# Seven-product blocks of a feed-forward stage: the plain product on the lower left weights third, the outputs of the block ahead in front of the sixth product

## The chip, the cores and the metric

The kernel runs on one core of one Trainium2 chip. The metric is the device time of one execution in microseconds, the median of several runs. All times below are in microseconds unless marked ns.

## The reference

A decoder trunk of two layers over 256 tokens of width 1024. Each layer is a feed-forward network (FFN), an attention, and a second FFN; the first layer's attention is of the stick-breaking kind, the second's a sliding window of 128 with sinks, whose keys and values come from the stream after the first layer. The FFN, which this study is about, is

```
def swiglu(x, w_in, w_out):
    gate, up = jnp.split(x @ w_in, 2, axis=-1)
    return (jax.nn.silu(gate) * up) @ w_out

h = h + 0.5 * swiglu(rms_norm(h, norm), w_in, w_out)     # four times
```

with `w_in` of 1024 x 5632 and `w_out` of 2816 x 1024, all float32. The four FFNs are most of the work.

## The kernel before

**Precision.** Every float32 weight is split into two parts: ACT casts it to `w_hi` (L418), DVE subtracts that from the original and writes the rest as `w_lo` (L420), each in two halves of 128 x 1024. Operands are split the same way (`xT`, `S_h` and `S_l`, `aT_h` and `aT_l`). A *step* is three matmuls of 128 x 512 (operand high on w_hi, operand low on w_hi, operand high on w_lo). A product has four steps.

**Blocks.** An FFN goes through its 2816 hidden columns in blocks. The first blocks are of a plain or a narrow kind; the others, 512 columns wide, use Strassen's scheme, in which the two token tiles, the two halves of the 1024 inputs and gate and up form a 2 x 2 by 2 x 2 product. Four weight tiles of 1 MB are loaded for such a block, r11 and r21 (gate, upper and lower half of the inputs; r21 holds the lower left weights) and r12 and r22 (up). Seven products replace eight. The first FFN has four such blocks, the other three five each, 19 in all. The numbers by which the code calls the products are used here: before the change they run in the order 1, 5, 3, 2, 6, 7, 4.

- Product 1: r11, plain, into PSUM bank a. Its result is copied for later use, in most blocks into bank b (L797).
- DVE adds r12 to r11 (`add`, L610). Product 5: r11 on the operand sum S0, into bank d. ACT copies the result to the tile p5 (`stage`, L781).
- Product 3: r22 on S3, added into bank d.
- Product 2: r21, plain, into bank b. ACT's silu of that gives the gate s1 of the first token tile.
- Product 6: r11 (by then r11 + r12 + r22) on S1, added into bank a. ACT copies bank a to u2; DVE adds bank d to u2 (`plus`, L785) and multiplies with s1 (L788); PE transposes the result (L676), ACT and DVE split it into aT_h and aT_l.
- Product 7: r12 (by then r12 + r22) on S2, added into bank a. DVE adds bank a to p5 (`plus`, L785).
- Product 4: r11, plain, added into bank a; silu of that times p5 is the second token tile's half.

The sum r12 + r22, and the lower left weights that are added to r11 for product 4, are made by an accumulating DMA from POOL's queue (`fetch`, L615); the other two sums are made by DVE.

**Outputs.** A finished block's aT_h and aT_l are multiplied with two 1 MB tiles of `w_out` in 16 steps (8 for a narrow block) that accumulate over the FFN in four banks. `between()` places the output steps of the block ahead; before the change it stands between product 7 and product 4. The last two blocks' outputs stand behind the last block.

**Order.** Each instruction is recorded as a task with a duration, a place and what it reads and writes; a list planner then decides the order on each engine. PE's tasks have the order of the code as their rank, but when the first in rank isn't ready, PE takes the next that is. Hence a piece of a later product or of the outputs can stand between two products. Tasks of other engines are ranked by when they are due. The resulting order is fixed when the program is built; on the chip each engine's queue waits at its first instruction that isn't ready. Weight tiles pass through six raw slots and ten slots (five pairs) for w_hi and w_lo; a slot is handed on in the order of the code.

Of the kernel before, what the change touches and what calls it, by code (L numbers as in the profile page):

```python
# [18 lines left out]
D = 1024  # L19
# [20 lines left out]
PIECES = 2  # L40
ADDING = 170.0
PLAIN = 330.0
BY_DMA = False
DMA3 = True
FSUMS = 5000.0
TM = 1000.0
BOOST = 10000.0
# [11 lines left out]
LATE = (True, True, True)  # L59
KVFIRST = True  # L60
KVLATE = 3000.0
C11_0 = False
BL_LATE = 0.0

# [149 lines left out]
def dve(n):  # L214
    return n / 0.96 + 70
# [11 lines left out]
def kernel(  # L227
# [34 lines left out]
    RAW, WP, A4 = Slots("raw", RAWS, 8), Slots("w", HL, 8), Slots("a", 4, 4)  # L262
# [17 lines left out]
    def ts(t):  # L280
        return slice(t * P, (t + 1) * P)
# [7 lines left out]
    def B(*bs):  # L289
        return [(b, 0) for b in bs]  # L290
# [109 lines left out]
    def flat(buf):  # L400
        return buf.ap.rearrange("p a b -> p (a b)")
# [3 lines left out]
    def split(raw, prio=None):  # L405
        prio = plan.pos - LEAD if prio is None else prio
        a, b = raw.ab
        if raw.cut == 4:
            return split_fine(raw, prio)
        hi, lo = WP.get([P, a, b], F32R, "w_hi"), WP.get([P, a, b], F32R, "w_lo")  # L410
        m = a * b // PIECES
        for j in range(PIECES):
            sl = slice(j * m, (j + 1) * m)
            ks = [j] if PIECES == 2 else [0, 1]
            rs = [2 * j, 2 * j + 1] if raw.cut == 4 else ks

            first = [(xh, (0, 0))] if raw.cut == 4 and j == 1 else []
            T("ACT", act(m), lambda sl=sl: ACT.copy(out=flat(hi)[:, sl], in_=flat(raw)[:, sl]),  # L418
              r=[(raw, i) for i in rs] + first, w=[(hi, i) for i in ks], prio=prio)
            T("DVE", dve(m), lambda sl=sl: DVE.tensor_sub(out=flat(lo)[:, sl], in0=flat(raw)[:, sl],  # L420
                                                          in1=flat(hi)[:, sl].bitcast(F32)),
              r=[(raw, i) for i in rs] + [(hi, i) for i in ks], w=[(lo, i) for i in ks], prio=prio)
        return hi, lo
# [22 lines left out]
    def by_k(w):  # L446
        return w.rearrange("(k p) n -> p k n", p=P)
# [23 lines left out]
    def of_x(t, k):  # L471
        return ((lambda: xh.ap[:, k, ts(t)], lambda: xl.ap[:, k, ts(t)]), [(xh, (t, k // 4)), (xl, (t, k // 4))])
# [129 lines left out]
    def of_sums(SH, SL, i):  # L602
        return lambda kk: ((lambda: SH.ap[:, i, kk], lambda: SL.ap[:, i, kk]), [(SH, i), (SL, i)])

    def add(dst, src):
        m = 2048 // PIECES
        for i in range(PIECES):
            sl = slice(m * i, m * i + m)
            ks = [i] if PIECES == 2 else [0, 1]
            T("DVE", dve(m), lambda sl=sl: DVE.tensor_add(out=flat(dst)[:, sl], in0=flat(dst)[:, sl], in1=flat(src)[:, sl]),  # L610
              r=[(src, k) for k in ks], w=[(dst, k) for k in ks], prio=plan.pos - LEAD)


    def fetch(dst, src):
        T("POOL", 1500, lambda: nc.gpsimd.dma_start(out=dst.ap, in_=src, accum_op=ALU.add), w=[(dst, 0), (dst, 1)],  # L615
          prio=plan.pos - LOADS, lat=500.0)
        T("SP", P * 2048 * 4 / ADDING, lambda: None, w=[(dst, 0), (dst, 1)], prio=plan.pos - LOADS)

    def product(bank, raw, xs, first, last, at=0.0):
        w = split(raw)  # L620
        for kk in range(4):
            step(bank, w, kk, xs(kk), first and kk == 0, last and kk == 3)
        WP.put(*w)

    def ffn(w_in, w_out, acc, rest, finish, kv=None, blocks=BLOCKS, roots=None, ending=False, there=False, arranged=False):

        first, late = arranged, roots is not None
        wi, wo = by_k(w_in), by_k(w_out)  # L630
        wi4 = w_in.rearrange("(j p k) n -> p j k n", j=2, k=4)
        ring = [banks[i] for i in rest[0:3]]
# [16 lines left out]
        def of_s(i):  # L649
            return of_sums(SH, SL, i)  # L650

        def col(h, i, c, n=512):
            cs = slice(h * DFF + c, h * DFF + c + n)
            return wi4[:, i, :, cs] if first else wi[:, 4 * i:4 * i + 4, cs]

        def silu(dst, src, r, w, t, n=512):
            if late:
                T("ACT", act(n, True), lambda: ACT.activation(out=dst(), in_=src(), func=AF.Silu, scale=roots[t][0].ap), r=r + B(roots[t][0]) + [(consts, "tbl")], w=w)
            else:
                T("ACT", act(n), lambda: ACT.activation(out=dst(), in_=src(), func=AF.Silu), r=r + [(consts, "tbl")], w=w)  # L660
# [9 lines left out]
        def turn(m, t, aT, nk=4):  # L670
            n = nk * P
            view = lambda b: (lambda: b.ap[:, 0:nk, ts(t)])

            def run():
                for i in range(nk):
                    PE.transpose(out=tr.ap[:, i * P:(i + 1) * P], in_=m.ap[:, i * P:(i + 1) * P], identity=ident)  # L676
            T("PE", 109 * nk, run, r=B(m) + ID, w=B(tr))
            STG.put(m)
            part_to(tr, (aT[0], t, view(aT[0])), (aT[1], t, view(aT[1])), n,
                    lambda: tr.ap[:, 0:n].rearrange("p (a b) -> p a b", a=nk))  # L680
# [92 lines left out]
        def strassen(n, c, between):  # L773
            a, d, b = ring
            ring[:] = [d, b, a]
            aT = new_a()
            r11, r12, r22, r21 = [load([(slice(0, 512), col(h, i, c))], 4, 512) for h, i in ((0, 0), (1, 0), (1, 1), (0, 1))]

            def stage(src, name):
                s = STG.get([P, 512], F32, name)  # L780
                T("ACT", act(512), lambda: ACT.copy(out=s.ap, in_=src.ap), r=B(src), w=B(s), prio=plan.pos - STAGE)  # L781
                return s

            def plus(s, bank):
                T("DVE", dve(512), lambda: DVE.tensor_add(out=s.ap, in0=s.ap, in1=bank.ap), r=B(bank), w=B(s))  # L785

            def mul_less(dst, a_, b_, r, w, t):
                T("DVE", dve(512), lambda: DVE.scalar_tensor_tensor(out=dst(), in0=b_(), scalar=roots[t][1].ap if late else -1.0, in1=a_(),  # L788
                                                                    op0=ALU.mult, op1=ALU.mult),
                  r=r + (B(roots[t][1]) if late else []), w=w, lat=LAT["DVE"] + TM)  # L790

            product(a, r11, lambda kk: of_x(0, kk), True, False)
            c11 = C11 and (n != 1 or blocks[0] == "p" or C11_0)
            if c11:
                T("ACT", act(512), lambda: ACT.copy(out=b.ap, in_=a.ap), r=B(a), w=B(b), prio=plan.pos - STAGE)  # L797
                s1 = STG.get([P, 512], F32, "s1")
            else:
                s1 = stage(a, "s1")  # L800
            add(r11, r12)
            product(d, r11, of_s(0), True, False)
            p5 = stage(d, "p5")
            if BY_DMA:
                fetch(r11, col(1, 1, c))
            else:
                add(r11, r22)
            if DMA3:
                fetch(r12, col(1, 1, c))
            else:  # L810
                add(r12, r22)
            product(d, r22, of_s(3), False, True)
            RAW.put(r22)
            product(b, r21, lambda kk: of_x(0, 4 + kk), not c11, True)
            RAW.put(r21)
            if c11:
                silu(lambda: s1.ap, lambda: b.ap, B(b), B(s1), 0)
            else:
                plus(s1, b)
                silu(lambda: s1.ap, lambda: s1.ap, [], B(s1), 0)  # L820
            product(a, r11, of_s(1), False, False)
            fetch(r11, col(0, 1, c))
            u2 = stage(a, "u2")
            plus(u2, d)
            mul_less(lambda: s1.ap, lambda: s1.ap, lambda: u2.ap, B(u2), B(s1), 0)
            STG.put(u2)
            turn(s1, 0, aT)
            product(a, r12, of_s(2), False, False)
            RAW.put(r12)
            plus(p5, a)  # L830
            between()
            product(a, r11, lambda kk: of_x(1, 4 + kk), False, True)
            RAW.put(r11)
            m = STG.get([P, 512], F32, "m")
            silu(lambda: m.ap, lambda: a.ap, B(a), B(m), 1)
            mul_less(lambda: m.ap, lambda: m.ap, lambda: p5.ap, B(p5), B(m), 1)
            STG.put(p5)
            turn(m, 1, aT)
            return aT, 4
# [300 lines left out]
    def shared_kv(vec, other):  # L1140
# [25 lines left out]
        def run(ring, tr):  # L1166
# [19 lines left out]
            at_ = plan.pos  # L1186
            plan.pos += KVLATE
            for t in range(NT):
# [404 lines left out]
```

## Time and profile before

| | |
|---|---|
| median of 3 runs | 911.37 (910.37 to 911.4) |
| the profiled execution, and its span | 910.39, span 908.6 |
| first FFN, 19 to 185 | PE busy 166.00 of 166.00, DVE 148.04, DMA 0.93 |
| second FFN, 290 to 475 | PE 185.00 of 185.00, DVE 174.79, DMA 0.86 |
| third FFN, 475 to 662 | PE 186.44 of 187.00, DVE 174.90, DMA 0.89 |
| fourth FFN, 722 to the end | PE 178.97 of 186.60, DVE 171.46, DMA 0.74 |

PE is the engine of the matrix products (PEld its weight loads), DVE and ACT the vector and scalar engines, POOL and SP issue DMAs. A row of the timeline holds the start, the length, the engine, the line of the kernel, the operation, the output and inputs by their names in the program, and in brackets how long the engine stood idle before and what ended that. Two tiles are called p and u there: p5 and u2 with their numbers left out. A matmul's end is modelled, so consecutive matmuls overlap in the rows, and a short wait is seen in the distance of their starts.

### The profile page before, as it was taken

The page shows a single profiled execution, that of the slowest core. Times are in us where ns is not written, and L with a number is a line of the kernel's source. Part 1 is how long each engine was busy: PE and PEld are TensorE (multiplying, and loading weights), DVE is VectorE, ACT ScalarE, POOL GpSimd, SP SyncE. Part 2 cuts the span into 40 slices and gives each one's busy share as a digit, 9 for nine tenths or more (in the row PEclk, how much of TensorE's full clock was granted, in tenths as well). Part 3 has the DMA queues.
Part 4 walks back from the last instruction along what each step waited for, and adds up shares of the span by engine and source line. Part 5 has one row for each costly group of instructions (what it writes and reads, how often), then busy time and mean ns, then how long its engine had stood idle before and what let it go on. Part 6 is the DMA issues. An engine that isn't in the chain of part 4 may idle for free.

```text
span 908.6 us, 11840 instructions
## 1 busy us (share of the span) xinstructions
PE 897.5 (99%) x4420; PEld 739.5 (81%) x4420; DVE 818.3 (90%) x989; ACT 650.1 (72%) x935; POOL 66.7 (7%) x71
## 2 busy tenths in 40 slices
PE   9999999999999999999999999999999999999997
PEld 6888888888888888888888878888897787788886
DVE  8989989687977999998889999999788799999985
ACT  7867667786986876776688767667857677677662
POOL 2001000000000101010000101010000001101000
PEclk9999999999999999999999999999999999999999
DMA  9997999995763499999795999998944149999951
GB/s 337 349 238 223 289 298 233 285 291 154 239 206 115 104 267 306 246 290 268 211 343 127 255 264 266 284 318 225 335 129 163 47 107 287 284 250 291 323 148 47
DMA packets 107305, 214.43 MB, mean 236 GB/s; under 512 B 6256, under 2 KB 27760, under 8 KB 107248
## 3 DMA queue, kind: packets, MB, share of 16 engines
q1 hardware_dynamic: 85184, 170.49, 52.6%
q0 software_dynamic: 21648, 42.99, 26.9%
q8 instruction: 34, 0.56, 0.2%
q10 hardware_dynamic: 416, 0.20, 0.1%
q14 instruction: 23, 0.19, 0.1%
HBM read 212.62 MB, written 1.05 MB: 235 GB/s over the span
## 4 chain that ended last, share of the span: by engine, by line
PE 89%; DVE 8%; ACT 2%; issue 1%; DMA 0%; DVEq 0%; ACTq 0%
PE ps L287 85%; DVE w_lo L420 4%; PE ps L676 2%; ACT w_hi L418 1%; PE ps L490 1%; DVE raw L610 1%; DVE e L1319 0%; PE ps L1327 0%; DMA hN<-in_x_dram 0%; DVE s L586 0%; DVE small L1293 0%; DVE S_l L580 0%; ACT u L781 0%; DVE aT_l L497 0%; DVE o_l L1359 0%
## 5 line engine op out<-in xcount | busy, mean ns | idle before, releaser
L420 DVE TENSOR_TENSOR w_lo<-raw,w_hi 128x1024 fp32r<-128x1024 f32 x424 | 499.8, 1219 | 24.7 <-ACT w_hi L418 23.1
L418 ACT CAST w_hi<-raw 128x1024 fp32r<-128x1024 f32 x424 | 423.0, 1049 | 102.9 <-DVE raw L610 40.0
L287 PE MATMUL ps<-w_hi,xT 128*128 128x512 f32 (+1 forms) x788 | 229.8, 375 | 0.0
L287 PEld LDWEIGHTS ps<-w_hi,xT 128*128 128x128 f32 x788 | 142.7, 188 | 26.6 <-DVE xT L497 0.5
L287 PE MATMUL ps<-w_lo,xT 128*128 128x512 f32 (+1 forms) x394 | 146.8, 373 | 0.0
L287 PE MATMUL ps<-w_hi,aT_h 128*128 128x512 f32 x354 | 139.9, 395 | 0.0
L287 PE MATMUL ps<-w_lo,aT_h 128*128 128x512 f32 x354 | 137.7, 389 | 0.0
L287 PE MATMUL ps<-w_hi,aT_l 128*128 128x512 f32 x354 | 137.5, 388 | 0.0
L287 PE MATMUL ps<-w_hi,S_h 128*128 128x512 f32 x320 | 127.3, 398 | 2.0 <-ACT u L781 1.2
L287 PE MATMUL ps<-w_lo,S_h 128*128 128x512 f32 x320 | 124.9, 390 | 0.0
L287 PE MATMUL ps<-w_hi,S_l 128*128 128x512 f32 x320 | 124.8, 390 | 0.0
L610 DVE TENSOR_TENSOR raw<-raw 128x1024 f32<-128x1024 f32 x78 | 94.6, 1220 | 0.5
L615 POOL DMA_DIRECT2D raw<-in_ffn_w_in_dram x38 | 48.3, 1271 | 507.2 <-DVE w_lo L420 255.3
L287 PEld LDWEIGHTS ps<-w_lo,xT 128*128 128x128 f32 x394 | 74.2, 188 | 13.6 <-DVE w_lo L420 0.4
L287 PEld LDWEIGHTS ps<-w_lo,aT_h 128*128 128x128 f32 x354 | 66.4, 188 | 13.9
L287 PEld LDWEIGHTS ps<-w_hi,aT_l 128*128 128x128 f32 x354 | 66.6, 188 | 13.0
L287 PEld LDWEIGHTS ps<-w_hi,aT_h 128*128 128x128 f32 x354 | 66.5, 188 | 12.8
L287 PEld LDWEIGHTS ps<-w_hi,S_h 128*128 128x128 f32 x320 | 60.1, 188 | 16.8 <-ACT u L781 3.2
L287 PEld LDWEIGHTS ps<-w_lo,S_h 128*128 128x128 f32 x320 | 60.1, 188 | 13.0 <-DVE w_lo L420 0.2
L287 PEld LDWEIGHTS ps<-w_hi,S_l 128*128 128x128 f32 x320 | 60.2, 188 | 11.5
L496 ACT CAST aT_h<-ps 128x512 fp32r<-128x512 f32 (+1 forms) x48 | 26.3, 549 | 49.4 <-PE ps L676 49.2
L287 PE MATMUL ps<-xT,w_hi 128*128 128x512 f32 (+1 forms) x136 | 47.0, 394 | 0.0
(184 smaller groups left out, 941.7 us busy)
## 6 DMA issues: line engine op xcount, KB each, us to landing
raw<-in_ffn_w_in_dram SPq DMA_DIRECT2D x76, 1024.0 KB, 7.5
raw<-in_ffn_w_out_dram SPq DMA_DIRECT2D x44, 1024.0 KB, 8.2
raw<-in_ffn_w_in_dram POOLq DMA_DIRECT2D x38, 1024.0 KB, 10.0
raw<-in_sb_w_qkv_dram SPq DMA_DIRECT2D x12, 1024.0 KB, 8.0
raw<-in_ffn_w_in_dram SPq DMA_DIRECT2D x16, 512.0 KB, 6.4
raw<-in_ffn_w_in_dram SPq DMA_DIRECT2D x16, 256.0 KB, 5.4
raw<-in_sb_w_o_dram SPq DMA_DIRECT2D x4, 1024.0 KB, 5.3
raw<-in_swa_w_q_dram SPq DMA_DIRECT2D x4, 1024.0 KB, 9.0
```

What stands on the lines that cost most here:

```text
L287: PE.matmul(ps, lhsT=lhsT, rhs=rhs, start=start, stop=stop, skip_group_check=True)
L418: T("ACT", act(m), lambda sl=sl: ACT.copy(out=flat(hi)[:, sl], in_=flat(raw)[:, sl]), r=[(raw, i) for i in rs] + first, w=[(hi, i) for i i ...
L420: T("DVE", dve(m), lambda sl=sl: DVE.tensor_sub(out=flat(lo)[:, sl], in0=flat(raw)[:, sl], in1=flat(hi)[:, sl].bitcast(F32)), r=[(raw, i) ...
L490: PE.matmul(bank.ap[:, i * P:(i + 1) * P], lhsT=s, rhs=ident, start=i == 0, stop=True, is_transpose=True, skip_group_check=True)
L496: T("ACT", act(n), lambda: ACT.copy(out=hi[2](), in_=src()), r=B(bank), w=[hi[0:2]])
L610: T("DVE", dve(m), lambda sl=sl: DVE.tensor_add(out=flat(dst)[:, sl], in0=flat(dst)[:, sl], in1=flat(src)[:, sl]), r=[(src, k) for k in ks ...
L615: T("POOL", 1500, lambda: nc.gpsimd.dma_start(out=dst.ap, in_=src, accum_op=ALU.add), w=[(dst, 0), (dst, 1)], prio=plan.pos - LOADS, lat=5 ...
L676: PE.transpose(out=tr.ap[:, i * P:(i + 1) * P], in_=m.ap[:, i * P:(i + 1) * P], identity=ident)
```

## The change

A table `SPECIAL`, keyed by the FFN and the block, gives for each seven-product block who makes the four sums (V for DVE, D for an accumulating DMA), which of products 2 and 3 goes first, and in front of which product the outputs of the block ahead stand. All 19 blocks get the same entry. The makers stay as they were. Product 2 goes third and product 3 fourth, and `between()` stands in front of product 7 instead of product 4. The products now run in the order 1, 5, 2, 3, 6, (outputs), 7, 4. The raw slots of r21 and r22 are handed on in the new order too.

```diff
-BY_DMA = False
-DMA3 = True
...
+SPECIAL = {(f, n): ('VVDD', (2, 3), 7) for f in (1, 2, 3, 4) for n in range(1, 6)}
...
-            add(r11, r12)
+            makers, second, filled = SPECIAL.get((len(stage_), n), ("VVDD", (3, 2), 4))
+
+            def fill(q):
+                if q == filled:
+                    between()
...
+            summed(0, r11, r12, 1, 0)
             product(d, r11, of_s(0), True, False)
             p5 = stage(d, "p5")
...
-            product(d, r22, of_s(3), False, True)
-            RAW.put(r22)
-            product(b, r21, lambda kk: of_x(0, 4 + kk), not c11, True)
-            RAW.put(r21)
+            summed(1, r11, r22, 1, 1)
+            summed(2, r12, r22, 1, 1)
+            for q in second:
+                if q == 3:
+                    product(d, r22, of_s(3), False, True)
+                    RAW.put(r22)
+                else:
+                    product(b, r21, lambda kk: of_x(0, 4 + kk), not c11, True)
+                    if makers[3] == "D":
+                        RAW.put(r21)
...
+            fill(6)
             product(a, r11, of_s(1), False, False)
-            fetch(r11, col(0, 1, c))
+            summed(3, r11, r21, 0, 1)
...
             turn(s1, 0, aT)
+            fill(7)
             product(a, r12, of_s(2), False, False)
             RAW.put(r12)
             plus(p5, a)
-            between()
+            fill(4)
             product(a, r11, lambda kk: of_x(1, 4 + kk), False, True)
```

(Lines L286, L419, L496, L609, L787 and L790 of the changed kernel are L287, L420, L497, L610, L785 and L788 of the one before.) What the planner makes of it, on PE, in the second seven-product block of the fourth FFN. Before, product 3 (w_hi_6283) follows product 5 (w_hi_6304) at once:

```order
L287 MATMUL ps_66<-w_hi_6304,S_h_6099 128x512
L287 MATMUL ps_66<-w_hi_6304,S_l_6117 128x512
L287 MATMUL ps_66<-w_lo_6320,S_h_6099 128x512
L287 MATMUL ps_66<-w_hi_6283,S_h_6099 128x512
L287 MATMUL ps_66<-w_hi_6283,S_l_6117 128x512
L287 MATMUL ps_66<-w_lo_6359,S_h_6099 128x512
```

and now, after product 5 (w_hi_6312), the ahead block's product 4 (w_hi_6341):

```order
L286 MATMUL ps_66<-w_hi_6312,S_h_6099 128x512
L286 MATMUL ps_66<-w_hi_6312,S_l_6117 128x512
L286 MATMUL ps_66<-w_lo_6325,S_h_6099 128x512
L286 MATMUL ps_66<-w_hi_6341,xT_163 128x512 x2
L286 MATMUL ps_66<-w_lo_6355,xT_163 128x512
```

Four steps of it, and only then product 3; in most other blocks the four steps are product 2's, of which two stood there before. Further on in the same block, on PE before, product 7 (w_hi_6411) behind product 6 (w_hi_6406):

```order
L287 MATMUL ps_66<-w_hi_6406,S_h_6099 128x512
L287 MATMUL ps_66<-w_hi_6406,S_l_6117 128x512
L287 MATMUL ps_66<-w_lo_6423,S_h_6099 128x512
L287 MATMUL ps_66<-w_hi_6411,S_h_6099 128x512
L287 MATMUL ps_66<-w_hi_6411,S_l_6117 128x512
L287 MATMUL ps_66<-w_lo_6451,S_h_6099 128x512
```

and now, behind product 6 (w_hi_6395), output steps (aT), nine in all up to product 7:

```order
L286 MATMUL ps_66<-w_hi_6395,S_h_6099 128x512
L286 MATMUL ps_66<-w_hi_6395,S_l_6117 128x512
L286 MATMUL ps_66<-w_lo_6413,S_h_6099 128x512
L286 MATMUL ps_66<-w_hi_6363,aT_h_6293 128x512
L286 MATMUL ps_66<-w_hi_6363,aT_l_6400 128x512
L286 MATMUL ps_66<-w_lo_6423,aT_h_6293 128x512
```

Between products 7 and 4, where 14 output steps and the transpose of s1 stood in a block in the middle of an FFN, there are now steps of the next block's product 1: two in three blocks, three in ten (and three output steps in one), and more, of either kind, in five.

On DVE, in the second seven-product block of the second FFN, the add to p5 stood before behind the u2 and s1 operations and the split of a `w_out` tile (w_hi_2922), far ahead of product 4's split (w_hi_2993):

```order
L785 TENSOR_TENSOR u2_2936<-u2_2936,ps_66 128x512
L788 SCALAR_TENSOR_TENSOR s1_2911<-u2_2936,small_67,s1_2911 128x512
L497 TENSOR_TENSOR aT_l_2829<-ps_66,aT_h_2772 128x4x128
L420 TENSOR_TENSOR w_lo_2957<-raw_2859,w_hi_2922 128x1024 x2
L785 TENSOR_TENSOR p5_2861<-p5_2861,ps_66 128x512
L420 TENSOR_TENSOR w_lo_2979<-raw_2909,w_hi_2947 128x1024
```

It now stands between the two halves of product 4's split (w_hi_3019), behind the splits of the next block's products 1 and 5 (w_hi_2944, w_hi_2997) and ahead of its product 2 (w_hi_3042):

```order
L419 TENSOR_TENSOR w_lo_2977<-raw_2885,w_hi_2944 128x1024 x2
L609 TENSOR_TENSOR raw_2885<-raw_2885,raw_2913 128x1024 x2
L496 TENSOR_TENSOR aT_l_3007<-ps_66,aT_h_2972 128x4x128
L419 TENSOR_TENSOR w_lo_3014<-raw_2885,w_hi_2997 128x1024 x2
L419 TENSOR_TENSOR w_lo_3031<-raw_2483,w_hi_3019 128x1024
L787 TENSOR_TENSOR p5_2864<-p5_2864,ps_66 128x512
L419 TENSOR_TENSOR w_lo_3031<-raw_2483,w_hi_3019 128x1024
L419 TENSOR_TENSOR w_lo_3052<-raw_3002,w_hi_3042 128x1024 x2
```

The add has moved from ahead of product 4's split into it, and later on PE's clock. The number of instructions on each engine is the same in both programs.

More of the change, by code (lines that the diff above doesn't have):

```diff
@@ L623, in product @@
         WP.put(*w)
+    stage_ = []
     def ffn(w_in, w_out, acc, rest, finish, kv=None, blocks=BLOCKS, roots=None, ending=False, there=False, arranged=False):
         first, late = arranged, roots is not None
+        stage_.append(0)
         wi, wo = by_k(w_in), by_k(w_out)
@@ L800, in strassen, with summed @@
                 s1 = stage(a, "s1")
-            add(r11, r12)
+            makers, second, filled = SPECIAL.get((len(stage_), n), ("VVDD", (3, 2), 4))
+            def fill(q):
+                if q == filled:
+                    between()
+            def summed(i, dst, src, h, k):
+                if makers[i] == "D":
+                    fetch(dst, col(h, k, c))
+                else:
+                    add(dst, src)
+            summed(0, r11, r12, 1, 0)
             product(d, r11, of_s(0), True, False)
             p5 = stage(d, "p5")
[L804 to L811, printed above, removed]
-            product(d, r22, of_s(3), False, True)
-            RAW.put(r22)
-            product(b, r21, lambda kk: of_x(0, 4 + kk), not c11, True)
-            RAW.put(r21)
+            summed(1, r11, r22, 1, 1)
[4 more added lines that the diff above has]
+                    RAW.put(r22)
+                else:
+                    product(b, r21, lambda kk: of_x(0, 4 + kk), not c11, True)
+                    if makers[3] == "D":
+                        RAW.put(r21)
             if c11:
@@ L820, in strassen @@
                 silu(lambda: s1.ap, lambda: s1.ap, [], B(s1), 0)
+            fill(6)
             product(a, r11, of_s(1), False, False)
-            fetch(r11, col(0, 1, c))
+            summed(3, r11, r21, 0, 1)
+            if makers[3] != "D":
+                RAW.put(r21)
             u2 = stage(a, "u2")
```

## The prediction

> **What bounds the kernel now.** The engine table of the page comes first, then the same busy times for one stretch in the middle of the second feed-forward stage, where every block has its seven products.
>
> ```profile
> span 908.6 us, 11840 instructions
> PE   897.5 (99%) x4420; PEld 739.5 (81%) x4420; DVE 818.3 (90%) x989; ACT 650.1 (72%) x935; POOL 66.7 (7%) x71
> ...
> core 0: us, PE busy (x) PEld busy (x) DVE busy (x) ACT busy (x) POOL busy (x), PEclk, DMA share, GB/s
> 350.00:440.00 90.00, 90.00 (x410) 74.36 (x409) 86.95 (x85) 62.72 (x74) 7.68 (x6) 1.00 0.96 279
> ```
>
> PE has no gap at all there, DVE is busy for 86.95 of 90 us and the DMA engines for 0.96. The change adds and removes no instruction, so it can only move PE's waits. The view of waits, for PE alone, says how many are marked:
>
> ```profile
> PE ps L287 <- ACT u L781: 1.2, 2, 0.7
> PE ps L287 <- ACT p L781: 0.7, 1, 0.7
> ```
>
> Both are copies out of a PSUM bank that the next product adds to. Since a matmul's end is modelled, short stalls hide inside "busy" and must be read from the starts. Here is the one behind ACT p, from the timeline (start, length):
>
> ```profile
> 769.68 0.39 PE L287 MATMUL ps<-w_hi,S_l 128*128 128x512 f32 x1
> 769.91 0.39 PE L287 MATMUL ps<-w_lo,S_h 128*128 128x512 f32 x1
> 770.33 0.59 ACT L781 COPY p<-ps 128x512 f32<-128x512 f32 x1
> 770.97 0.50 PE L287 MATMUL ps<-w_hi,S_h 128*128 128x512 f32 x1 [0.68 <-ACT p L781]
> 771.31 0.39 PE L287 MATMUL ps<-w_hi,S_l 128*128 128x512 f32 x1
> ```
>
> The normal pitch of two matmuls is 0.23. Product 5 ends, ACT copies its bank to p5, and product 3, which adds into that bank, starts 1.06 after the last matmul: 0.83 lost, and the next pitch is 0.34, another 0.11. That is 0.94 us, and it is the whole price of an uncovered copy.
>
> **The change, part by part.** *What goes.* The same search for pitches over 0.23 in the seven-product blocks finds five more stalls at the places that the change reorders. Four are between products 6 and 7, where u2 is copied from the bank that product 7 adds to:
>
> ```profile
> 781.15 0.39 PE L287 MATMUL ps<-w_lo,S_h 128*128 128x512 f32 x1
> 781.57 0.59 ACT L781 COPY u<-ps 128x512 f32<-128x512 f32 x1 [1.04 <-PE ps L287]
> 782.21 0.50 PE L287 MATMUL ps<-w_hi,S_h 128*128 128x512 f32 x1 [0.68 <-ACT u L781]
> 782.55 0.39 PE L287 MATMUL ps<-w_hi,S_l 128*128 128x512 f32 x1
> 783.13 0.68 DVE L785 TENSOR_TENSOR u<-u,ps 128x512 f32<-128x512 f32 x1
> ...
> 533.41 0.39 PE L287 MATMUL ps<-w_lo,aT_h 128*128 128x512 f32 x1
> 533.71 0.57 ACT L781 COPY u<-ps 128x512 f32<-128x512 f32 x1
> 534.33 0.50 PE L287 MATMUL ps<-w_hi,S_h 128*128 128x512 f32 x1 [0.54 <-ACT u L781]
> 534.67 0.40 PE L287 MATMUL ps<-w_hi,S_l 128*128 128x512 f32 x1
> 535.08 0.68 DVE L785 TENSOR_TENSOR u<-u,ps 128x512 f32<-128x512 f32 x1
> ...
> 347.53 0.59 ACT L781 COPY u<-ps 128x512 f32<-128x512 f32 x1
> 347.78 0.39 PE L287 MATMUL ps<-w_lo,aT_h 128*128 128x512 f32 x1
> 348.17 0.50 PE L287 MATMUL ps<-w_hi,S_h 128*128 128x512 f32 x1
> 348.51 0.40 PE L287 MATMUL ps<-w_hi,S_l 128*128 128x512 f32 x1
> 349.02 0.68 DVE L785 TENSOR_TENSOR u<-u,ps 128x512 f32<-128x512 f32 x1
> ...
> 813.00 0.39 PE L287 MATMUL ps<-w_lo,aT_h 128*128 128x512 f32 x1
> 813.51 0.50 PE L287 MATMUL ps<-w_hi,S_h 128*128 128x512 f32 x1
> 813.84 0.39 PE L287 MATMUL ps<-w_hi,S_l 128*128 128x512 f32 x1
> ```
>
> By the same subtraction: 0.83 + 0.11 at 781; 0.69 + 0.11 at 533; 0.16 + 0.11 at 347; 0.28 + 0.10 at 813. Where the first matmul behind the copy is preceded by one on aT_h, the planner had put one or two output steps of 0.68 (three matmuls) between, and ACT was simply late. The fifth is a second p5 copy, with two steps of product 2 as cover:
>
> ```profile
> 587.61 0.57 ACT L781 COPY p<-ps 128x512 f32<-128x512 f32 x1
> 587.83 0.39 PE L287 MATMUL ps<-w_lo,xT 128*128 128x512 f32 x1
> 588.24 0.50 PE L287 MATMUL ps<-w_hi,S_h 128*128 128x512 f32 x1
> 588.58 0.40 PE L287 MATMUL ps<-w_hi,S_l 128*128 128x512 f32 x1
> ```
>
> 0.18 + 0.11. All six: 0.94 + 0.94 + 0.80 + 0.27 + 0.38 + 0.29 = 3.62 us. In the other blocks the planner already covers both copies, so nothing is to be had there. Afterwards four steps (2.7 us) of another product stand between products 5 and 3, and in most blocks eight or sixteen output steps between 6 and 7; I take the whole 3.62 as gone, with 0 to 0.3 left over where output steps are few (the last block of a stage has two or three).
>
> *What comes.* Product 4 now follows product 7 directly in the code, both in one bank, and between them DVE must add that bank to p5. Uncovered this costs 0.39 for the last matmul, 0.03 until the reader starts, 0.68 for the add (the u add in the rows above has the same shape), 0.05 until PE starts, less one pitch of 0.23: 0.92, and 0.11 behind it. The new order covers it with the next block's product 1: two steps (1.36 us) in 3 of the 19 blocks, three (2.04) in 11 (one of them with output steps), more in 5. So the add may start 0.44 late with two steps and 1.12 late with three before PE waits. How late such an add starts today is read at the u add against the end of the u copy: 0.90 at 347, 0.80 at 533, 0.97 at 781 (rows above), and at the two ends
>
> ```profile
> 439.89 0.59 ACT L781 COPY u<-ps 128x512 f32<-128x512 f32 x1 [0.73 <-PE ps L287]
> ...
> 440.73 0.68 DVE L785 TENSOR_TENSOR u<-u,ps 128x512 f32<-128x512 f32 x1
> ...
> 753.58 0.57 ACT L781 COPY u<-ps 128x512 f32<-128x512 f32 x1
> ...
> 753.71 2.35 DVE L420 TENSOR_TENSOR w_lo<-raw,w_hi 128x1024 fp32r<-128x1024 f32 x2
> 755.98 0.68 DVE L785 TENSOR_TENSOR s<-s,ps 128x512 f32<-128x512 f32 x1
> 756.58 0.68 DVE L785 TENSOR_TENSOR u<-u,ps 128x512 f32<-128x512 f32 x1
> ```
>
> 0.25 and 2.43, the latter behind two weight splits (1.13 each, start to start) and another add. The usual case is one split in progress, so a delay anywhere from 0 to 1.13. With two steps of cover that is on average 0.69 x 0.69 / 2 / 1.13 = 0.21, and with the restart about 0.28; three blocks, 0.8. With three steps one split fits, and only a queue like the last one costs, 2.43 - 1.12 + 0.11 = 1.4; I allow a third of one such case, 0.4. The ends are 0, if DVE always stands ready at the add, and for fourteen blocks at 2.43 each 3 x 2.1 + 11 x 1.4 = 22. I take 1.2, near the low end, since four of the five delays lie under 1.0. Behind the waiting add on DVE stand the second half of product 4's own split and product 2's of the next block; product 4 reaches the second half only after two steps, 1.36, and the split takes 1.22, so it just hides.
>
> [...]
>
> *What moves.* The lower left weights are split one place earlier. In most blocks the first half of them was used there before, as cover for p5, so a late load costs nothing new; 0 to 0.3. The weight for it is loaded into the slot that the second output weight leaves, not the first, one split later (2.3 us) in some thirteen. Product 7's accumulating load gets more time, product 4's stays as far behind product 6. The planner also shifts a few rows in both attention stages, where nothing was changed: 0 to 0.3 either way. For all of these I put 0.3.
>
> **Sum.** -3.62 + 1.2 + 0.3 = -2.1 us. The profiled execution took 910.39 (span 908.6), so 908.3; the median shown, 911.37, is 1.0 above it, so **909.3**. A difference under 0.2%, 1.8 us, can't be told from none here.
>
> **Rivals.** *The cover was mostly there and the new wait pays back the rest* (the change hardly does what it says). The six stalls lie in five blocks, the other fourteen show none; were the add 0.9 late, as at 347, 533 and 781, in the three two-step blocks (0.46 + 0.11 each, 1.7) and like 753 in one three-step block (1.4), with 0.3 moved, the net is -0.2: 911.2. For it: four of five delays lie above the 0.44. Against: the add now stands where the order expects its input, not behind the u add. Chance 0.37.
>
> *Slower: DVE reaches the p5 add late in block after block.* DVE has 3 us to spare in 90, and its queue is in order, as the rows at 753 show. It decides where the mean wait over the fourteen blocks passes 3.6 / 14 = 0.26, that is, an add some 1.3 late with three steps, two splits ahead of it. At two splits (2.27) in half of them the price is (3 x 1.94 + 11 x 1.26) / 2 = 9.8, net +6.2 or more: 917.6. Against: those 3 us, some 1 us in each block of 30, and that DVE falls into step with PE again at every add that waits for it. Chance 0.13. [...]
>
> **How the numbers follow.** Forecast 0.50, no visible change 0.37, slower 0.13; these are also the chances of the three signs. The likeliest case reaches from 907.5 (all 3.62 gone, nothing new) to 909.5; the second up to about 913. The range for eight in ten is 907.4 to 912.4, leaving out the slower rival and the edges.
>
> **What would show it.** Right: no pitch over 0.3 between products 5 and 3 or 6 and 7 except single 0.09 ones; the waits of PE on ACT u and ACT p gone; a few waits of PE on DVE p, each under 0.8, three at most above 0.3. Wrong: PE waiting for DVE p in ten or more blocks; a marked wait on w_lo or w_hi at product 2; a stage that lengthens without such a wait.

## The result and the profile after

The changed kernel took **922.12 us** (median of 4 runs, 921.06 to 922.74), the kernel before 911.06 beside it (910.37 to 911.4): ratio 1.0125, 95% interval 1.0112 to 1.0137. It is slower by 11 us, where 909.3 was forecast, and outside the range. The profiled execution took 922.74, its span 921.0 against 908.6. From the page of the changed kernel, the span, PE's busy time and the granted clock in 40 slices:

```profile
span 921.0 us, 11858 instructions
PE 901.8 (98%) x4420; PEld 742.7 (81%) x4420; DVE 818.8 (89%) x989; ACT 650.2 (71%) x935; POOL 66.6 (7%) x71
...
PEclk9999999999999999999999999999999999989999
```

One slice, 806 to 829 us, shows an 8: the clock was down there for a while. The view of PE's waits (in total, times, longest) says what PE stood for:

```profile
PE ps L286 <- ACT w_hi L417: 8.3, 3, 4.8
PE ps L286 <- DVE p L787: 1.5, 2, 1.0
```

The waits on ACT u and ACT p are gone, as forecast. A wait on split weights has come, of a kind that is not in the list of before; two of the three, 7.6 of the 8.3 us, are in FFN4.

Product 5 of FFN4's second seven-product block starts, in the trace of before, at

```profile
764.49 0.39 PE L287 MATMUL ps<-w_hi,S_h 128*128 128x512 f32 x1
```

and after it would start at 766.26 (one pitch behind the first row below): up to there the change has cost 1.8 us net. The other 10.6 of the 12.4 us of span come behind it, in two stalls of that one block. The first, in the timeline of the changed kernel (start, length, and in brackets the idle time before and what ended it):

```profile
766.03 0.39 PE L286 MATMUL ps<-w_lo,xT 128*128 128x512 f32 x1
766.27 7.68 ACT L417 CAST w_hi<-raw 128x1024 fp32r<-128x1024 f32 x8 [5.40 <-DMA raw<-in_ffn_w_in_dram]
...
769.26 0.77 PE L286 MATMUL ps<-w_hi,S_h 128*128 128x512 f32 x1 [2.84 <-ACT w_hi L417]
769.83 0.63 PE L286 MATMUL ps<-w_hi,S_l 128*128 128x512 f32 x1
```

PE waits for product 5's weight, whose sum DVE had begun at 761.26. But ACT's order has product 2's split ahead of product 5's (w_hi_6299 ahead of w_hi_6312), and ACT stood idle for 5.40 us until r21, the weight of product 2, had landed. Then came two halves for product 2 and one for product 5, 3.0 us, and PE lost just that. The view of transfers, around their issue (KB, us to landing), says why r21 was late:

```profile
raw<-in_ffn_w_in_dram POOLq DMA_DIRECT2D x1, 1024.0 KB, 11.5
raw<-in_ffn_w_in_dram SPq DMA_DIRECT2D x1, 1024.0 KB, 11.3
```

POOL's row is the accumulating load for product 4 of the block ahead, issued at 753.50; SP's is r21, issued at 754.90. They share the engines: from 755 to 765 the packets of POOL's queue took 62% of the time of the 16 DMA engines, for 1.05 MB, and those of SP's 37%, for 1.38 MB. The two loads land nearly together, at 765.0 and 766.2. The second stall is in front of product 4 (rows of PE, POOL, ACT and DVE, in order of start):

```profile
789.44 1.26 POOL L614 DMA_DIRECT2D raw<-in_ffn_w_in_dram  x1 [22.88 <-DVE w_lo L419]
...
802.60 0.39 PE L286 MATMUL ps<-w_lo,xT 128*128 128x512 f32 x1
...
804.72 5.78 ACT L417 CAST w_hi<-raw 128x1024 fp32r<-128x1024 f32 x6 [5.26 <-DMA raw<-in_ffn_w_in_dram]
...
805.79 1.22 DVE L419 TENSOR_TENSOR w_lo<-raw,w_hi 128x1024 fp32r<-128x1024 f32 x1 [4.56 <-ACT w_hi L417]
806.93 0.68 DVE L787 TENSOR_TENSOR p<-p,ps 128x512 f32<-128x512 f32 x1
...
807.76 1.19 PE L286 MATMUL ps<-w_hi,xT 128*128 128x512 f32 x2 [4.77 <-ACT w_hi L417]
```

PE stops for 4.93 us. The load for product 4 is issued at 789.44 and lands 15.3 us later (row below), at 804.7; ACT splits it at once. The profile puts the whole wait down to that split. But the first half of w_hi was there at 805.8, and PE started 2 us later, 0.15 behind the add to p5 (806.93 + 0.68 = 807.61). The add needs only product 7, whose last matmul was over by 800.3; it stands on DVE behind the first half of product 4's own split, and so behind the load. The transfer of that load, after; then before, with POOL's issue and product 4's first matmuls:

```profile
raw<-in_ffn_w_in_dram POOLq DMA_DIRECT2D x1, 1024.0 KB, 15.3
```

```profile
780.21 1.26 POOL L615 DMA_DIRECT2D raw<-in_ffn_w_in_dram  x1 [15.61 <-DVE w_lo L420]
...
raw<-in_ffn_w_in_dram POOLq DMA_DIRECT2D x1, 1024.0 KB, 10.5
...
797.80 0.62 PE L287 MATMUL ps<-w_hi,xT 128*128 128x512 f32 x2
```

Before, that load went out at 780.21, 17.6 us ahead of product 4 (797.80), and took 10.5. After, it had 13.4 us (789.44 to 802.83, where product 4 would have started) and took 15.3. It waits for the second half of product 6's split, which the planner now does late: the output steps in front of product 7 lie between the halves of product 6, and their own splits, on ACT half of product 7's too, go between the halves on ACT and DVE.

The stalls cost more than their length. Windows of the changed kernel, cut at the stalls (PE's busy time, and the granted clock in the third column from the end):

```profile
757.00:766.00 9.00, 9.00 (x43) 7.45 (x42) 7.70 (x8) 0.59 (x1) 0.71 (x1) 1.00 1.07 299
766.00:769.10 3.10, 0.42 (x2) 0.00 (x0) 0.00 (x0) 2.83 (x3) 0.56 (x1) 1.00 0.73 167
769.10:775.00 5.90, 5.56 (x15) 3.72 (x16) 5.69 (x6) 5.65 (x8) 0.00 (x0) 0.71 0.77 141
...
807.60:815.00 7.40, 7.24 (x20) 5.81 (x21) 5.57 (x7) 4.60 (x7) 0.00 (x0) 0.59 0.76 210
```

After each stall the clock is low: 15 matmuls in 5.90 us, 20 in 7.40, where the pitch of 0.227 would have let 26 and 32 pass. With that, and a short wait for w_lo, the first stall costs 5.4 us and the second 7.8 (matmul starts against the pitch). Behind the first, the pitch is 0.43 from 771.11 to 772.39, 1.9 times the usual; the gap there was 2.84 us between a matmul's modelled end and the next start, 3.23 from start to start. The two stalls together cost 13.2 us, more than the 10.6, because 2.3 come back behind the same point: the stalls of before at 769, 781 and 813 (0.94, 0.94 and 0.38) are gone. The small rest was not traced.

### The profile page after: what moved, and what is told of

The parts are those of the page before. It is cut to its first block, busy times and chain, and to the rows that moved or that the text cites. A ratio compares the mean times of both kernels' runs of the same rounds, so it can differ in the third digit from the quotient of the medians.

```text
span 921.0 us, 11858 instructions
## 1 busy us (share of the span) xinstructions
PE 901.8 (98%) x4420; PEld 742.7 (81%) x4420; DVE 818.8 (89%) x989; ACT 650.2 (71%) x935; POOL 66.6 (7%) x71
## 3 DMA queue, kind: packets, MB, share of 16 engines
HBM read 212.62 MB, written 1.05 MB: 232 GB/s over the span
## 4 chain that ended last, share of the span: by engine, by line
PE 72%; issue 9%; DVE 9%; DMA 7%; ACT 2%; POOL 0%; POOLq 0%; DVEq 0%; ACTq 0%
PE ps L286 69%; DMA raw<-in_ffn_w_in_dram 6%; DVE w_lo L419 4%; ACT w_hi L417 2%; PE ps L678 2%; DMA raw<-in_ffn_w_out_dram 1%; PE ps L489 1%; DVE raw L609 1%; DVE xs L1453 0%; DVE e L1336 0%; DVE hN L566 0%; PE ps L1344 0%; DVE s L585 0%; DVE xT L496 0%; DVE S_l L579 0%
## 5 line engine op out<-in xcount | busy, mean ns | idle before, releaser
L419 DVE TENSOR_TENSOR w_lo<-raw,w_hi 128x1024 fp32r<-128x1024 f32 x424 | 498.6, 1219 | 27.3 <-ACT w_hi L417 25.9
L286 PE MATMUL ps<-w_hi,xT 128*128 128x512 f32 (+1 forms) x788 | 233.6, 381 | 7.0 <-ACT w_hi L417 5.5
L286 PEld LDWEIGHTS ps<-w_hi,xT 128*128 128x128 f32 x788 | 142.2, 190 | 35.5 <-ACT w_hi L417 8.3
L286 PE MATMUL ps<-w_lo,xT 128*128 128x512 f32 (+1 forms) x394 | 148.1, 376 | 0.1
L286 PE MATMUL ps<-w_hi,aT_h 128*128 128x512 f32 x354 | 139.9, 395 | 0.0
L286 PE MATMUL ps<-w_lo,aT_h 128*128 128x512 f32 x354 | 137.7, 389 | 0.0
L286 PE MATMUL ps<-w_hi,aT_l 128*128 128x512 f32 x354 | 137.5, 388 | 0.0
L286 PE MATMUL ps<-w_hi,S_h 128*128 128x512 f32 x320 | 126.2, 394 | 2.8 <-ACT w_hi L417 2.8
L286 PE MATMUL ps<-w_lo,S_h 128*128 128x512 f32 x320 | 125.3, 391 | 0.1
L286 PE MATMUL ps<-w_hi,S_l 128*128 128x512 f32 x320 | 125.2, 391 | 0.0
L609 DVE TENSOR_TENSOR raw<-raw 128x1024 f32<-128x1024 f32 x78 | 94.0, 1219 | 0.4
L286 PEld LDWEIGHTS ps<-w_lo,xT 128*128 128x128 f32 x394 | 74.7, 190 | 14.1 <-DVE w_lo L419 0.5
L286 PEld LDWEIGHTS ps<-w_lo,aT_h 128*128 128x128 f32 x354 | 66.5, 188 | 13.9
L286 PEld LDWEIGHTS ps<-w_hi,aT_l 128*128 128x128 f32 x354 | 66.6, 188 | 12.8
L286 PEld LDWEIGHTS ps<-w_hi,aT_h 128*128 128x128 f32 x354 | 66.5, 188 | 12.7
L286 PEld LDWEIGHTS ps<-w_hi,S_h 128*128 128x128 f32 x320 | 60.6, 189 | 15.7 <-ACT w_hi L417 3.3
L286 PEld LDWEIGHTS ps<-w_lo,S_h 128*128 128x128 f32 x320 | 60.4, 189 | 13.5 <-DVE w_lo L419 0.8
L286 PEld LDWEIGHTS ps<-w_hi,S_l 128*128 128x128 f32 x320 | 60.7, 190 | 12.4
L286 PE MATMUL ps<-xT,w_hi 128*128 128x512 f32 (+1 forms) x136 | 47.0, 394 | 0.0
```

Source lines behind the costliest of these rows:

```text
L286: PE.matmul(ps, lhsT=lhsT, rhs=rhs, start=start, stop=stop, skip_group_check=True)
```

## The experiments

The two halves of the change come first, each alone in all stages, then the stages. Theory A was: the loss is FFN4's, and comes from the outputs in front of product 7.

```
e1_swap   ('VVDD', (2, 3), 4)  for f in (1, 2, 3, 4)
e2_outs   ('VVDD', (3, 2), 7)  for f in (1, 2, 3, 4)
e3_f123   ('VVDD', (2, 3), 7)  for f in (1, 2, 3)
```

> One half of the change alone: products in the order 1, 5, 2, 3, 6, 7, 4, outputs in front of product 4 as before. Theory A (the loss comes from the outputs moved in front of product 7: with them the planner puts the split of a block's third product ahead of product 5's in the fourth FFN, and ACT's queue then stands at a weight that has not landed): no wait of PE for w_hi over 1 us, 909 to 911.5. Rival (the lower left weights, loaded last and now needed third, are late wherever they go third): the stalls of 3.0 and 4.9 us in the fourth FFN are there, 918 to 922.

Measured 910.45 (before beside these runs: 911.69), ratio 0.9979, 0.9968 to 0.999.

> The other half alone: products 1, 5, 3, 2, 6 as before, outputs in front of product 7. Theory A: both stalls in the fourth FFN are there, 918 to 923. Rival (lower left weights third): they are gone, 910 to 913.

Measured 917.79, ratio 1.0063 (1.0048 to 1.0078): just under what was expected.

> The whole change in the first three FFNs, the fourth as before. By the changed kernel's trace the first three end 1.8 us later than before (waits of 1.15, 0.85 and 0.69 us for the add to p5) and the rest of the 11 us falls in the fourth: 912 to 913.5, if the fourth's loss is its own. If it is inherited from a shifted start: 918 or more.

Measured 911.45, ratio 0.9992 (0.9982 to 1.0002), a little under what was expected. So the move of the outputs does the harm, the move of product 2 alone does none, and FFN4 alone loses; in FFN 1 to 3 the whole change is worth nothing that can be told. But the two halves do not add up: product 2 on top of the outputs costs 4.3 us more. A rule on ACT's order was the next test: in FFN4, ACT's copies for products 3 and 2 also wait for those of product 5.

```
- r=[(raw, i) for i in rs] + first
+ r=[(raw, i) for i in rs] + first + list(behind)
...
+ fifth = product(d, r11, of_s(0), True, False)
...
+ product(d, r22, of_s(3), False, True, behind=fifth)
+ product(b, r21, lambda kk: of_x(0, 4 + kk), not c11, True, behind=fifth)
```

> The whole change, but in the fourth FFN the planner may not put the splits of products 2 and 3 ahead of that of the same block's product 5; PE's order there stays the same. Theory A1 (ACT's queue standing at the late weight is the first cause, and the second stall follows from the lead lost in the first): both go, 910 to 914. Theory A2 (two causes; the accumulating load of product 4 is late because seven output steps stand between the halves of product 6): the first stall of 3.0 and its slow matmuls, 4.9 us together, go, the second stays, 916 to 918. Rival: neither goes, 920 to 923.

Measured 916.45, ratio 1.0048 (1.0034 to 1.0063). The first stall is gone; its waits on w_hi are

```profile
PE ps L286 <- ACT w_hi L417: 5.2, 2, 4.6
```

and on ACT product 5's halves are now done when DVE has them, with no wait for r21:

```profile
762.64 1.05 ACT L417 CAST w_hi<-raw 128x1024 fp32r<-128x1024 f32 x1 [1.69 <-DVE raw L609]
764.98 4.85 ACT L417 CAST w_hi<-raw 128x1024 fp32r<-128x1024 f32 x5 [1.28 <-DVE raw L609]
```

So the first stall is worth about 922.12 - 916.45 = 5.7 us (the interval of e4_behind is 1.3 us to either side), as its 5.4 said, and the second stands by itself. For that one, the splits of the output weights were held behind product 6's in FFN4, with and without the rule on product 2:

```
+ held[:] = product(a, r11, of_s(1), False, False)
...
+ return weight([(slice(0, D), wo[:, k:k + 2, :])], 2, D, behind=held)
```

> The whole change, with two rules added for FFN4: the splits of products 2 and 3 may not be placed ahead of product 5's (as in e4_behind), and no split of a second weight may be placed before both halves of product 6's split, so that the accumulating load for product 4 is issued early. The output steps then follow product 6 as one group in the second seven-product block. Theory A (two separate causes in FFN4, a late load that holds up ACT's queue, about 5 us, and the accumulating load of product 4 issued late, about 7 us): both stalls gone, the load for product 4 issued at least 4 us earlier against its product, 910.5 to 913.5 us. Rival B (the outputs in front of product 7 leave too little time for that load wherever its split stands, since it shares the DMA engines with three others): a wait of over 2 us in front of product 4 stays, 915 to 919 us.

> The whole change, with only the second of the two rules of e5_both: no split of a second weight ahead of both halves of product 6's split in FFN4. It moves the planner's order ahead of product 5 too, and ends with nearly the order of e5_both, without a rule on products 2 and 3. Theory A: within 1 us of e5_both, 910.5 to 914 us. If the first stall needs the rule on products 2 and 3 itself, it comes back (3 us of waiting for w_hi and slow matmuls behind it): 915 to 918 us.

Measured 911.65 (ratio 1.0004, 0.999 to 1.0017) and 912.12 (1.0005, 0.9992 to 1.0018); before beside these runs 911.48. Both stalls are gone in both; the longest wait left for weights is 1.2 us, for w_lo. In e6_hold POOL issues the load at

```profile
781.00 1.26 POOL L614 DMA_DIRECT2D raw<-in_ffn_w_in_dram  x1 [16.21 <-DVE w_lo L419]
...
797.73 0.70 PE L286 MATMUL ps<-w_hi,xT 128*128 128x512 f32 x2 [0.45 <-DVE p L789]
```

16.7 us ahead of product 4 in place of 13.4. Of the wait 0.45 is left, the add's. The load is 3.3 us earlier, a little less than the 4 expected. The planner also gave product 5 another place there, so these two show that the loss is not in the order of the products as such, but don't separate the two stalls.

> The whole change, except in the second seven-product block of FFN4, which has the entry of before (product 3 ahead of product 2, outputs in front of product 4). Theory A (the loss is made where four loads meet in that block, and nowhere else): 911 to 913.5 us, no wait for w_hi over 1.5 us in FFN4. Rival C (the change makes FFN4 as a whole late on its loads, the second block being only where it shows first): the loss comes back in the third block, 916 to 922 us.

Measured 912.61 (1.0009, 0.9996 to 1.0022): with that block alone as before, the loss is gone and does not come back later. Rival C falls. The other side of the race is the load itself, here without its adding:

```
- fetch(dst, col(h, k, c))
+ fetch(dst, col(h, k, c), not (len(stage_) == 4 and i == 3))
```

> The whole change in the same order; in FFN4 the load for product 4 overwrites its weight tile and does not add to it (so product 4 there computes with the upper weights left out). Theory A says that the 15.3 us of this load are its late place among three other loads on the shared DMA engines: it still lands 13 us or more after its issue, a wait of over 3 us in front of product 4 stays, 920 to 923 us. Rival D (it is the adding that makes the load slow): it lands within 10 us, the wait in front of product 4 is gone or under 1 us, 914 to 916 us.

Measured 909.61 (0.9982, 0.9972 to 0.9992). Theory A as put here was wrong, and D right, beyond its own number. The pair that had taken 11.5 and 11.3 took

```profile
raw<-in_ffn_w_in_dram POOLq DMA_DIRECT2D x1, 1024.0 KB, 5.6
raw<-in_ffn_w_in_dram SPq DMA_DIRECT2D x1, 1024.0 KB, 7.3
```

The load that does not add took half the time (5.6 in place of 11.5 us), and the plain load beside it was quicker too (7.3 in place of 11.3), which is why the first stall went as well. The same edit on the kernel before says whether that is a gain of its own:

> The kernel before, with the same edit of FFN4's load for product 4 as e9_plain (it overwrites its tile and does not add, so product 4 there computes with the upper weights left out). If the change is neutral but for the slow load, and a quick load takes its loss away: the kernel before has no wait on that load, so it gains little, 909.5 to 911.5 us, and stands within 1 us of e9_plain (909.61). If a quick load would have helped the kernel before as much as it helped the changed one: 900 to 903 us.

Measured 910.29 against 911.10, ratio 0.9998 (0.9988 to 1.0007): it gains nothing there. So the load's length costs only where the order gives it too little time; the place in the order and the length are both needed for the stall.

```
- ADDING = 170.0
+ ADDING = 90.0
```

> The whole change; one number of the planner is altered, so that it reckons 11.7 us of transfer for an adding load in place of 6.2 us (in the trace of the changed kernel such loads took 8.5 to 15.3 us from issue to landing). Theory: the loss is that the order leaves the load for product 4 less time than it takes beside three others; a planner that reckons more leaves more room: no wait for w_hi over 1.5 us in FFN4, 910 to 914 us. If room cannot be made in this order, or is taken from other loads: 915 us or more, with other waits for w_hi.

Measured **968.02**, ratio 1.0636 (1.0614 to 1.0658), far from the theory's 910 to 914; the other case, 915 or more, has no upper end. The planner made another program of it: PE waits 31 times for w_lo, 15.8 us in all, and 8 times for w_hi, 9.1 us. It tells nothing for or against the theory, except that this number is no way to make room; where its 57 us go was not followed up.

> The whole change in FFN 1 to 3, and in FFN4 product 2 third with the outputs left in front of product 4. Theory A: the loss needs the outputs in front of product 7 in FFN4, so it is gone; 910 to 911.5 us. A version that beats both kernels would be under 910.0.

> The kernel of e1_swap again, for a narrower interval: product 2 third in all blocks, outputs in front of product 4 as before. 910.0 to 911.0 us, 0.1 to 0.3% below the kernel before; same if the first interval's upper end (0.999) was luck.

Measured 910.45 (0.9992, 0.9983 to 1.0001) and 910.68 (0.9996, 0.9987 to 1.0005). The first interval of e1_swap, below 1, did not repeat: no version here that computes the same sums is faster than before by more than can be told. Last, the add to p5. Its place was changed alone, in FFN4, with PE's order in the block the same:

```
- r=[(raw, i) for i in rs] + [(hi, i) for i in ks], w=[(lo, i) for i in ks]
+ r=[(raw, i) for i in rs] + [(hi, i) for i in ks] + list(low), w=[(lo, i) for i in ks]
...
- product(a, r11, lambda kk: of_x(1, 4 + kk), False, True)
+ product(a, r11, lambda kk: of_x(1, 4 + kk), False, True, low=B(p5) if len(stage_) == 4 else ())
```

> The whole change; in FFN4 alone, both halves of product 4's split on DVE stand behind the add to p5, not one half ahead of it. PE's order in the block with the stalls is unchanged. If the add behind the split is a part of the loss: the second stall falls from 4.93 to about 3.0 us, and with fewer slow matmuls behind it the time falls by 2 to 3.5 us, to 918.5 to 920 us. If the late load alone sets the stall: 921.5 to 923 us.

> e4_behind and e14_add together: the first stall is taken out by the rule on ACT, the add to p5 stands ahead of product 4's split. If the parts add up: 916.45 less 2 to 3.5 us, that is 913 to 914.5 us, with a stall of about 3 us left in front of product 4. If the late load alone sets the stall: 916 to 917 us.

Measured 919.41 (1.0093, 1.0075 to 1.0111) and 914.56 (1.0042, 1.003 to 1.0055), before beside them 911.1: the first as expected, the second 0.1 above it. In e14_add DVE does the add in time and then waits for the load:

```profile
799.44 0.67 DVE L787 TENSOR_TENSOR p<-p,ps 128x512 f32<-128x512 f32 x1
804.24 3.50 DVE L419 TENSOR_TENSOR w_lo<-raw,w_hi 128x1024 fp32r<-128x1024 f32 x3 [4.12 <-ACT w_hi L417]
```

The second stall falls to 3.1 us there (2.8 in e15_add4). The place of the add is worth 922.12 - 919.41 = 2.7, with the first stall taken out 916.45 - 914.56 = 1.9. What e15_add4 has left over before, 3.5 us, is mainly the late load: 2.8 of stall, and probably slow matmuls behind it (the mean granted clock of its profiled execution is 0.997, in the runs of before beside it 0.998 or 0.999). This also fits e2_outs, 4.3 us quicker than the whole change: there DVE does the add ahead of the split,

```profile
798.12 0.68 DVE L787 TENSOR_TENSOR p<-p,ps 128x512 f32<-128x512 f32 x1
802.39 2.36 DVE L419 TENSOR_TENSOR w_lo<-raw,w_hi 128x1024 fp32r<-128x1024 f32 x2 [3.60 <-ACT w_hi L417]
```

the second stall is 2.7, and the first block of waits comes to 2.7 in place of 5.4.

## Why the prediction was wrong

*What goes, -3.62.* Right. The stalls behind the u2 and p5 copies are gone from the list of waits, and no new one stands between products 5 and 3 or 6 and 7. A small one came in front of product 2 in FFN4's second block, 0.3 at 778.6: its bank must first hold the copy of product 1's result.

*What comes, +1.2.* The mechanism was right, but a second one came with it. In FFN 1 to 3 PE waits for the add to p5 in six places, for 1.15, 0.85, 0.69, 0.19, 0.12 and 0.11, and 0.08 behind each: 3.6 us. In the last four, 1.4 us, DVE was busy without a gap ahead of the add, which is the wait that the step priced. The first two, 2.2 us, are another. What the step overlooked: it named the half of product 4's split that stands behind the add, and not the half ahead of it. DVE can't do that half before the load lands, so one late load holds the add as well. The two, at the end of FFN1 and in the second seven-product block of FFN2 (rows of ACT, DVE and PE):

```profile
160.66 0.39 PE L286 MATMUL ps<-w_lo,aT_h 128*128 128x512 f32 x1
162.03 0.70 PE L286 MATMUL ps<-w_hi,xT 128*128 128x512 f32 x2 [0.99 <-DVE p L787]
...
158.99 2.00 ACT L417 CAST w_hi<-raw 128x1024 fp32r<-128x1024 f32 x2 [2.01 <-DMA raw<-in_ffn_w_in_dram]
161.21 0.68 DVE L787 TENSOR_TENSOR p<-p,ps 128x512 f32<-128x512 f32 x1
...
362.35 5.79 ACT L417 CAST w_hi<-raw 128x1024 fp32r<-128x1024 f32 x6 [1.13 <-DMA raw<-in_ffn_w_in_dram]
364.58 0.68 DVE L787 TENSOR_TENSOR p<-p,ps 128x512 f32<-128x512 f32 x1
365.41 0.71 PE L286 MATMUL ps<-w_hi,xT 128*128 128x512 f32 x2 [0.69 <-ACT w_hi L417]
```

ACT takes up the landed load at 158.99, 362.35 and, in FFN4's second block, 804.72; PE starts product 4 at 162.03, 365.41 and 807.76, 3.0 to 3.1 later each time: half a split on ACT, half a split on DVE, the add (1.05, 1.22 and 0.68 us). So where the load sets the pace, it needs its transfer and 3 us more between its issue and product 4. The three loads, issued at 146.54, 348.34 and 789.44, had 14.4, 16.2 and 13.4 us before product 4 was due; they needed 12.4 + 3.1, 14.0 + 3.1 and 15.3 + 3.0. The differences, 1.1, 0.9 and 4.9, are the three waits. In the last one the add's part is 1.9 of the 4.93 us, 1.9 to 2.7 of the time.

Of the 3.62, 1.36 lay in FFN 1 to 3, so 2.2 net came there, near the 1.8 that the trace shows up to FFN4's second block. In e3_f123, where FFN 1 to 3 are changed alone, the planner's order in them is a little different and 2.0 came; its time shows neither gain nor loss.

*What moves, +0.3.* This step failed, in two sentences. "A late load costs nothing new": in this block product 2 was not the cover for p5, four steps of the block ahead's product 4 were, and ACT's queue had product 2's split ahead of product 5's. r21 landed 11.3 us after its issue, and the wait showed at product 5, not at product 2 where the sign was looked for: 5.7 us. "Product 4's stays as far behind product 6": the product stays, but its load hangs on the second half of product 6's split, which the planner did later; 17.6 us of room became 13.4, and the transfer grew from 10.5 to 15.3. By the matmul starts the second stall, the add's part in it, cost 7.8 us (e8_not and e9_plain have neither stall).

*The rivals.* The slower rival had the sign and neither the place nor the price: DVE late at the add in block after block was not seen, one block with two late loads was. FFN 1 to 3 went as the rival with chance 0.37 said, the cover mostly there and the rest paid back. *The signs.* PE waits for DVE p in two marked places, far from ten, but the longer, marked 0.99, is over the 0.8 allowed. The sign "a marked wait on w_lo or w_hi" was the one that came.

What stays open: why the planner leaves this load so little room in FFN4's second block; e8_not shows that it is this block, not why. The expectation of e11_slower says that the planner reckons 6.2 us for such a transfer, and these loads took 8.3 to 15.3 in the changed kernel, so by its own sum 13.4 us may have been ample; no run shows that this is the reason. In the next block the load, issued at 821.95, took 8.6 and had 16.8 us or more (PE goes on to product 1's steps of the block behind at 838.78), and PE didn't wait.

## What to carry to other kernels

When products change places, follow each weight back to its transfer: what frees its tile, when that happens in the new order, and which transfers it then shares the engines with (r21 took 11.3 us beside an adding load and 7.3 beside one that does not add); a move that leaves a product where it was can still take its load's head start away. Reckon the load with all that stands behind its landing: here the transfer and 3 us. Look at what stands ahead of the urgent instruction on its engine's queue and whether that waits for a transfer: ACT stood for 5.40 us in front of product 2's split, with product 5's behind it. Where a wait is put down to one engine, compare its end with PE's start: here 1.9 of 4.93 us belonged to an add behind it on another.

## What the runs showed of the hardware

In the changed kernel an accumulating load of 1 MB took 8.3 us at best (issued at 116.30) and up to 15.3 beside three others (at 789.44); a plain load issued by POOL in its place took 5.6 in e9_plain, or 8.6 beside two or three others (at 784.08), and its neighbour was quicker as well (7.3 in place of 11.3 us). Two loads of different queues that were issued 1.4 us apart, at 753.50 and 754.90, landed 1.2 apart. And a PE gap of 2.84 us was followed by matmuls at about half pace (pitch 0.43 in place of 0.227), so that a stall of 3.0 us, with a short wait for w_lo, cost 5.4.
